# The last row tile of a feed-forward's second product as whole float32: a hybrid encoder on one Trainium2 core

## The chip, the core and the metric

The kernel runs on one core of a Trainium2 chip, in one launch. The metric is the device time of the launch in microseconds (us); the lower the better. A run is timed as a whole; beside it stands one profiled execution, whose trace gives every time of a single instruction in this text.

## The reference

Two layers of an encoder on 256 tokens of width 1024, all in float32. Cut to what matters here, a layer is

```python
def swiglu(x, w_in, w_out):
    h = x @ w_in                                   # 1024 x 5632
    gate, up = h[..., :D_FF], h[..., D_FF:]
    return (jax.nn.silu(gate) * up) @ w_out        # 2816 x 1024

x = layer_norm(ALPHA * x + 0.5 * swiglu(x, ffn1_w_in[l], ffn1_w_out[l]), ...)
mix = hybrid_mixer(x, ...)     # one input projection, two kinds of attention, one output projection
x = layer_norm(ALPHA * x + mix, ...)
x = layer_norm(ALPHA * x + 0.5 * swiglu(x, ffn2_w_in[l], ffn2_w_out[l]), ...)
```

So there are four feed-forwards. Each has a second product, `g @ w_out`, over D_FF = 2816 = 22 x 128 rows of `w_out`.

## The kernel before

**Split operands.** TensorE works here on a type called float32r, float32 of reduced precision. To keep precision, every operand of a large product is split in two: a high part (the value cast to float32r) and a low part (the value less its high part, cast again). A product is then the sum of three matmuls: high by high, high by low, low by high. For a weight tile of 128 rows and 1024 columns this is done by `Weights._make` (lines 64 to 76): a DMA on SyncE's queue brings the tile into a buffer `raw` (five buffers), ScalarE casts it into `wh` (line 74, nine buffers), VectorE subtracts into `wl` (line 75, nine buffers). Both are issued at low priority. `srcs` (lines 126 to 138) lists all weight tiles in the order of their use, and `W.get(i)` (lines 82 to 84) has the program name eight tiles more than the one asked for (`LOOK`); the DMAs go out in that order as buffers come free.

**A feed-forward** is `ffn` (lines 288 to 402). The first four column blocks of gate and up are made by `first` (line 301). The other 18 are made by `col` (lines 324 to 343): two PSUM tiles `hg` and `hu`, filled from 16 matmuls each (lines 334 and 335), are added up, put through Silu and multiplied, which gives `gv` (line 340), a block of 128 rows of g-transposed by 256 tokens in plain float32, in half of the buffer `tl`. Lines 342 (ScalarE) and 343 (VectorE) split it into `gs`, which holds all 22 blocks for the second product.

**The second product** runs over the 22 row tiles k of `w_out`, for two halves t of 128 tokens. `step` (lines 376 to 383) issues for one k and one t the three partial products into the accumulators `acc[t]`: two of 512 columns, but in the program's last feed-forward three for the second half (512, 256, 256). The first 15 tiles are taken for both halves at once. The last seven (`TAIL`) are taken for the first half, whose normalisation then starts, and afterwards for the second half; there the last three tiles (`SPLIT`) are taken accumulator by accumulator. Before the last three steps the first half of the normalised x is transposed for the next stage (`to_xt`, line 400).

**What sets the order.** TensorE's instructions run in the order in which the code issues them (`manual_schedule(engines={PE})`, line 112). For the other engines a planner orders the work at compile time, by the data that each instruction needs and by priority; it also decides which buffer of a pool a tile gets. Each engine then executes its list strictly in order. In the mixer TensorE's order is written out by hand in `ORDER` (lines 47 to 54). It begins with `P dk 0 1`, a part of the key projection, whose weights are the fifth tile behind the last one of `w_out`.

**Plain float32 elsewhere.** The attention's products of probabilities and values are not split: line 568 (`od<-vd,pTd`, 128 columns) and line 598 (`os<-vs,pTs`, 64 columns) multiply plain float32. `diff_pv` issues 8 such calls and runs four times, `swa_pv` issues 16 and runs four times.

Of the kernel before, what the change touches and what calls it, by code (L numbers as in the profile page):

```python
# [19 lines left out]
P = 128  # L20
# [4 lines left out]
JT = DFF // P  # L25
# [25 lines left out]
S d 1; P sq 0 1; A 0 0; S d 1; P sq 0 1; P sq 1 2; A 0 1; T sk 1; T sq 0; T sk 0; V 0; P sq 1 1; A 1 1;  # L51
A 1 0; S s 0; Y 0 0; P sq 1 1; G; O 0 1; V 1; S s 0; T sq 1; O 0 1; W 0 0; O 0 1; S s 1; W 0 1; W 0 2;
Y 1 0; S s 1; W 1 0; Y 0 1; O 0 1; O 1 1; O 0 2; W 1 1; W 1 2; O 0 2; Y 1 1; O 1 6; Z; O 1 1
"""


class Weights:


    def __init__(self, tc, pool, srcs):  # L60
        self.tc, self.nc, self.pool, self.srcs = tc, tc.nc, pool, srcs
        self.made = []

    def _make(self, i):
        nc = self.nc
        raw = self.pool.tile([P, 1024], F32, tag="raw", name=f"raw{i}", bufs=5)
        wh = self.pool.tile([P, 1024], F32R, tag="wh", name=f"wh{i}", bufs=9)
        wl = self.pool.tile([P, 1024], F32R, tag="wl", name=f"wl{i}", bufs=9)
        n = 512 if i == 0 else 1024
        for c in range(0, 1024, n):  # L70
            s = slice(c, c + n)
            nc.sync.dma_start(raw[:, s], self.srcs[i][:, s])
            with self.tc.high_priority(-LATER):
                nc.scalar.copy(wh[:, s], raw[:, s])  # L74
                nc.vector.tensor_tensor(wl[:, s], raw[:, s], wh[:, s].bitcast(F32), ALU.subtract)  # L75
        self.made.append((wh, wl))
# [11 lines left out]
def encoder_kernel(  # L88
# [22 lines left out]
    nc = tc.nc  # L111
# [10 lines left out]
    mm = nc.tensor.matmul  # L122
    dv = nc.vector


    srcs = []
    for l in range(DEPTH):
        srcs += [f1_b[l, k] for k in range(KT)]
        srcs += [f1_in[l, j, s] for j in range(JT - NB) for s in range(2)]
        srcs += [f1_out[l, k * P : (k + 1) * P, :] for k in range(JT)]  # L130
        for c in range(3):
            srcs += [m_in[l, c, q] for q in range(4)]
        srcs += [m_in2[l, q] for q in range(2)]
        srcs += [m_in[l, 3, q] for q in range(4)]
        srcs += [m_out[l, k * P : (k + 1) * P, :] for k in range(KT)]
        srcs += [f2_b[l, k] for k in range(KT)]
        srcs += [f2_in[l, j, s] for j in range(JT - NB) for s in range(2)]
        srcs += [f2_out[l, k * P : (k + 1) * P, :] for k in range(JT)]
    W = Weights(tc, wp, srcs)
    wi = 0  # L140


# [21 lines left out]
    for c in range(4):  # L164
        load_xt(c)
        W.upto(c + 1)
    x = []

    def load_x():
        for t in range(2):  # L170
            xt = xp.tile([P, D], F32, tag="x", name=f"x_in{t}")
            nc.sync.dma_start(xt, x_tok[t * P : (t + 1) * P, :])
            x.append(xt)
# [114 lines left out]
    def ffn(l, n, last=False):  # L288
        nonlocal wi
        nm = f"{l}{n}"  # L290
        gs = [gp.tile([P, 2, 2, SEQ], F32R, tag="g", name=f"g_{nm}_{q}") for q in range(JT // 2)]

        def first(ts, mid=None):

            hp = [[ps.tile([P, 512], F32, tag="b", name=f"hb_{nm}_{t}{s}") for s in range(2)] for t in ts]
            for k in range(KT):
                wh, wl = W.get(wi + k)
                for t, hb in zip(ts, hp):
                    for g, ww, e in ((0, wh, 0), (0, wl, 1), (1, wh, 2)):
                        for s in range(2):  # L300
                            mm(hb[s], xx[:, k, g, t, :], ww[:, 512 * s : 512 * s + 512],  # L301
                               start=(k == 0 and e == 0), stop=(k == KT - 1 and e == 2))
                if k == KT - 3 and mid is not None:
                    mid()
            out = []
            for t, hb in zip(ts, hp):
                sg = tp.tile([P, 512], F32, tag="tmp", name=f"sgb_{nm}_{t}")
                nc.scalar.activation(sg, hb[0], AF.Silu)
                gv = tp.tile([P, 512], F32, tag="tmp", name=f"gvb_{nm}_{t}")
                dv.tensor_tensor(gv, sg, hb[1], ALU.mult)  # L310
                out.append(gv)
            return out

        def first_t(gv, t):
            tr = ps.tile([P, 4, P], F32, tag="b", name=f"trg_{nm}{t}")
            for i in range(4):
                nc.tensor.transpose(tr[:, i, :], gv[:, i * P : (i + 1) * P], ident)
            for q in range(2):
                a = slice(t * P, (t + 1) * P)
                dh = gs[q][:, :, 0, a]  # L320
                nc.scalar.copy(dh, tr[:, 2 * q : 2 * q + 2, :])
                dv.tensor_tensor(gs[q][:, :, 1, a], tr[:, 2 * q : 2 * q + 2, :], dh.bitcast(F32), ALU.subtract)

        def col(j):
            nonlocal wi

            hs = [ps.tile([P, 2, SEQ], F32, tag="b", name=f"h{'gu'[s]}_{nm}_{j}") for s in range(2)]
            tl = tp.tile([P, 2, SEQ], F32, tag="tl", name=f"tl_{nm}_{j}", bufs=2)
            for s in range(2):
                wh, wl = W.get(wi)  # L330
                wi += 1
                for k in range(KT):
                    a = slice(k * P, (k + 1) * P)
                    mm(hs[s], wh[:, a], xx[:, k], start=(k == 0), stop=False)  # L334
                    mm(hs[s][:, 1, :], wl[:, a], xx[:, k, 0], start=False, stop=(k == KT - 1))  # L335
                nc.scalar.copy(tl[:, s], hs[s][:, 1, :])  # L336
                dv.tensor_tensor(tl[:, s], hs[s][:, 0, :], tl[:, s], ALU.add)  # L337
            nc.scalar.activation(tl[:, 0], tl[:, 0], AF.Silu)  # L338
            gv = tl[:, 1]
            dv.tensor_tensor(gv, tl[:, 0], gv, ALU.mult)  # L340
            q, jj = divmod(j, 2)
            nc.scalar.copy(gs[q][:, jj, 0, :], gv)
            dv.tensor_tensor(gs[q][:, jj, 1, :], gv, gs[q][:, jj, 0, :].bitcast(F32), ALU.subtract)

        first_x = l == 0 and n == 0
        if first_x:
            g0, g1 = first((0, 1))
        else:
            (g0,) = first((0,), lambda: to_xt(x[1], 1, f"x{nm}"))
            (g1,) = first((1,))  # L350
        wi += KT
        if not first_x:
            first_t(g0, 0)
        col(NB)
        if first_x:
            first_t(g0, 0)
        first_t(g1, 1)
        for j in range(NB + 1, JT):
            col(j)
            if first_x and j == NB + 2:  # L360
                load_x()
                rotary()
            if j == JT - 6:
                gb = load_gb(l, n)
                if n == 0:
                    load_mix(l)
        def cols(t, ws):
            out, o = [], 0
            for w in ws:
                out.append((slice(o, o + w), ps.tile([P, w], F32, tag="b", name=f"acc_{nm}_{t}{o}")))  # L370
                o += w
            return out

        acc = [cols(0, (512, 512)), cols(1, (512, 256, 256) if last else (512, 512))]

        def step(k, w, t, hs=None):
            wh, wl = w
            q, kk = divmod(k, 2)
            gh = gs[q][:, kk, 0, t * P : (t + 1) * P]
            gl = gs[q][:, kk, 1, t * P : (t + 1) * P]  # L380
            for g, ww, e in ((gh, wh, 0), (gh, wl, 1), (gl, wh, 2)):
                for s, a in acc[t] if hs is None else [acc[t][h] for h in hs]:
                    mm(a, g, ww[:, s], start=(k == 0 and e == 0), stop=(k == JT - 1 and e == 2))  # L383

        for k in range(JT - TAIL):
            w = W.get(wi)
            wi += 1
            for t in range(2):
                step(k, w, t)
        ws = []  # L390
        for k in range(JT - TAIL, JT):
            ws.append(W.get(wi))
            wi += 1
            step(k, ws[-1], 0)
        layer_norm(acc[0], 0, 0.5, gb, nm, last)
        todo = [(k, None) for k in range(JT - TAIL, JT - SPLIT)]
        todo += [(k, (h,)) for h in range(len(acc[1])) for k in range(JT - SPLIT, JT)]
        for i, (k, hs) in enumerate(todo):
            if i == len(todo) - TCUT and not last:
                to_xt(x[0], 0, f"y{nm}")  # L400
            step(k, ws[k - JT + TAIL], 1, hs)
        layer_norm(acc[1], 1, 0.5, gb, nm, last)
# [403 lines left out]
```

## Time and profile before

| | us |
|---|---|
| median of 3 runs (981.85 to 982.15) | 981.9 |
| the profiled execution | 980.99 |
| its span, first to last instruction | 978.8 |

The mean granted TensorE clock of the profiled execution was 0.998 of full speed. A page of the profile gives the busy time of each engine and, in 40 equal slices of the span, the share of each slice in tenths. PE is TensorE's matmuls, PEld its weight loads, DVE VectorE, ACT ScalarE, POOL GpSimd, SP SyncE (SPq its queue, which issues the DMAs). An instruction is named by its line in the kernel, its operation and its tiles, out<-in. Matmuls are pipelined, and their ends are modelled: the time from one start to the next tells what one costs, the shown length does not. The chain that ended last follows the work back from the last instruction, at each step to what released it; its rows give a start, a time, and what ran (x is the number of instructions).

### The profile page before, as it was taken

The page shows a single profiled execution, that of the slowest core. Times are in us where ns is not written, and L with a number is a line of the kernel's source. Part 1 is how long each engine was busy: PE and PEld are TensorE (multiplying, and loading weights), DVE is VectorE, ACT ScalarE, POOL GpSimd, SP SyncE. Part 2 cuts the span into 40 slices and gives each one's busy share as a digit, 9 for nine tenths or more (in the row PEclk, how much of TensorE's full clock was granted, in tenths as well). Part 3 has the DMA queues.
Part 4 walks back from the last instruction along what each step waited for, and adds up shares of the span by engine and source line. Part 5 has one row for each costly group of instructions (what it writes and reads, how often), then busy time and mean ns, then how long its engine had stood idle before and what let it go on. Part 6 is the DMA issues. An engine that isn't in the chain of part 4 may idle for free.

```text
span 978.8 us, 13934 instructions
## 1 busy us (share of the span) xinstructions
PE 966.7 (99%) x5199; PEld 820.0 (84%) x5199; DVE 664.6 (68%) x1057; ACT 510.5 (52%) x887; POOL 18.3 (2%) x30
## 2 busy tenths in 40 slices
PE   8999999999999999999999999999999999999997
PEld 5888888888888888888888888888888888888886
DVE  6886764698748766664587667548896587666534
ACT  4667553446745655553355555433575456555430
POOL 1000000000000000000000000000000000000000
PEclk9999999999999999999999999999999999999999
DMA  8885566365305755555376655563742176555511
GB/s 290 318 271 192 191 193 194 127 236 175 111 23 193 249 183 192 185 183 194 126 254 220 190 180 189 194 193 133 244 141 66 45 245 231 191 186 182 191 65 44
DMA packets 50323, 176.44 MB, mean 180 GB/s; under 512 B 5824, under 2 KB 7376, under 8 KB 50256
## 3 DMA queue, kind: packets, MB, share of 16 engines
q1 hardware_dynamic: 50192, 175.54, 53.9%
q8 instruction: 41, 0.67, 0.3%
q0 software_dynamic: 64, 0.02, 0.1%
q14 instruction: 26, 0.21, 0.1%
HBM read 174.48 MB, written 1.05 MB: 179 GB/s over the span
## 4 chain that ended last, share of the span: by engine, by line
PE 98%; DMA 1%; DVE 1%; SPq 0%; ACT 0%; issue 0%; DVEq 0%
PE acc L383 24%; PE hu L334 14%; PE hg L334 14%; PE hb L301 9%; PE hg L335 7%; PE hu L335 7%; PE ao L666 4%; PE ss L486 2%; PE os L598 1%; PE pj_sq L448 1%; DMA raw<-in_f_b_dram 1%; PE pj_sq L450 1%; PE pj_dq L450 1%; PE pj_dq L448 1%; PE pj_sq L449 1%; PE pj_dv L448 1%
## 5 line engine op out<-in xcount | busy, mean ns | idle before, releaser
L75 DVE TENSOR_TENSOR wl<-raw,wh 128x1024 fp32r<-128x1024 f32 (+1 forms) x317 | 385.4, 1220 | 206.5 <-ACT wh L74 203.2
L74 ACT CAST wh<-raw 128x1024 fp32r<-128x1024 f32 (+1 forms) x317 | 332.1, 1050 | 328.3 <-PE acc L383 126.8
L334 PE MATMUL hg<-xx,wh 128*128 128x512 f32 x576 | 206.3, 399 | 0.0
L334 PE MATMUL hu<-xx,wh 128*128 128x512 f32 x576 | 205.7, 398 | 0.0
L383 PE MATMUL acc<-wh,g 128*128 128x512 f32 (+1 forms) x748 | 192.7, 378 | 0.0
L335 PE MATMUL hg<-xx,wl 128*128 128x256 f32 x576 | 161.3, 280 | 0.0
L335 PE MATMUL hu<-xx,wl 128*128 128x256 f32 x576 | 161.3, 280 | 0.0
L383 PEld LDWEIGHTS acc<-wh,g 128*128 128x128 f32 x748 | 136.0, 188 | 25.9
L334 PEld LDWEIGHTS hu<-xx,wh 128*128 128x128 f32 x576 | 108.2, 188 | 26.5
L334 PEld LDWEIGHTS hg<-xx,wh 128*128 128x128 f32 x576 | 108.2, 188 | 26.1
L383 PE MATMUL acc<-wl,g 128*128 128x512 f32 (+1 forms) x374 | 111.4, 377 | 0.0
L335 PEld LDWEIGHTS hg<-xx,wl 128*128 128x128 f32 x576 | 108.8, 189 | 0.0
L335 PEld LDWEIGHTS hu<-xx,wl 128*128 128x128 f32 x576 | 108.7, 189 | 0.0
L383 PEld LDWEIGHTS acc<-wl,g 128*128 128x128 f32 x374 | 68.9, 188 | 13.2
L301 PE MATMUL hb<-wh,xx 128*128 128x512 f32 x256 | 70.8, 393 | 3.1 <-ACT wh L74 3.1
L301 PEld LDWEIGHTS hb<-wh,xx 128*128 128x128 f32 x256 | 47.9, 188 | 14.4 <-ACT wh L74 4.8
L301 PE MATMUL hb<-wl,xx 128*128 128x512 f32 x128 | 39.9, 392 | 0.5 <-DVE wl L75 0.5
L666 PE MATMUL ao<-wh,xx 128*128 128x512 f32 x128 | 37.7, 398 | 0.0
L340 DVE TENSOR_TENSOR tl<-tl 128x256 f32<-128x256 f32 x72 | 30.6, 425 | 9.5 <-ACT tl L338 2.4
L337 DVE TENSOR_TENSOR tl<-hu,tl 128x256 f32<-128x256 f32 x72 | 30.1, 418 | 0.5 <-ACT tl L336 0.5
L338 ACT ACTIVATE tl<-tl 128x256 f32<-128x256 f32 x72 | 30.3, 421 | 0.0
L337 DVE TENSOR_TENSOR tl<-hg,tl 128x256 f32<-128x256 f32 x72 | 30.1, 418 | 0.3 <-ACT tl L336 0.3
(184 smaller groups left out, 980.2 us busy)
## 6 DMA issues: line engine op xcount, KB each, us to landing
raw<-in_f_in_dram SPq DMA_DIRECT2D x144, 512.0 KB, 4.3
raw<-in_f_out_dram SPq DMA_DIRECT2D x88, 512.0 KB, 4.2
raw<-in_m_in_dram SPq DMA_DIRECT2D x36, 512.0 KB, 4.4
raw<-in_f_b_dram SPq DMA_DIRECT2D x31, 512.0 KB, 3.4
raw<-in_m_out_dram SPq DMA_DIRECT2D x16, 512.0 KB, 4.2
lng<-in_ln_g_dram SPq DMA_DIRECT2D x6, 512.0 KB, 5.6
lnb<-in_ln_b_dram SPq DMA_DIRECT2D x6, 512.0 KB, 5.9
xr<-in_x_tr_dram SPq DMA_DIRECT2D x4, 256.0 KB, 7.4
```

The source lines that it names most:

```text
L74: nc.scalar.copy(wh[:, s], raw[:, s])
L75: nc.vector.tensor_tensor(wl[:, s], raw[:, s], wh[:, s].bitcast(F32), ALU.subtract)
L301: mm(hb[s], xx[:, k, g, t, :], ww[:, 512 * s : 512 * s + 512], start=(k == 0 and e == 0), stop=(k == KT - 1 and e == 2))
L334: mm(hs[s], wh[:, a], xx[:, k], start=(k == 0), stop=False)
L335: mm(hs[s][:, 1, :], wl[:, a], xx[:, k, 0], start=False, stop=(k == KT - 1))
L337: dv.tensor_tensor(tl[:, s], hs[s][:, 0, :], tl[:, s], ALU.add)
L338: nc.scalar.activation(tl[:, 0], tl[:, 0], AF.Silu)
L340: dv.tensor_tensor(gv, tl[:, 0], gv, ALU.mult)
L383: mm(a, g, ww[:, s], start=(k == 0 and e == 0), stop=(k == JT - 1 and e == 2))
L448: mm(o, xx[:, k, 0, t, :], wh[:, s], start=(k == 0), stop=False)
L450: mm(o, xx[:, k, 1, t, :], wh[:, s], start=False, stop=(k == KT - 1))
L666: mm(acc[t][h], xx[:, k, g, t, :], ww[:, s], start=(k == 0 and e == 0), stop=(k == KT - 1 and e == 2))
```

## The change

For the last row tile, k = 21, of each of the four second products nothing is split. The weight tile stays in its `raw` buffer, and no `wh` and `wl` are made; the column block `gv` stays in `tl`, and lines 342 and 343 are left out for it. `step` then issues one matmul for each accumulator, with both operands in plain float32, instead of three on float32r parts.

```diff
@@ class Weights
+        self.whole = set()
 
     def _make(self, i):
         nc = self.nc
         raw = self.pool.tile([P, 1024], F32, tag="raw", name=f"raw{i}", bufs=5)
+        if i in self.whole:
+            nc.sync.dma_start(raw, self.srcs[i])
+            self.made.append((raw,))
+            return
         wh = self.pool.tile([P, 1024], F32R, tag="wh", name=f"wh{i}", bufs=9)
         wl = self.pool.tile([P, 1024], F32R, tag="wl", name=f"wl{i}", bufs=9)
...
-    srcs = []
+    srcs, whole = [], []
     for l in range(DEPTH):
...
         srcs += [f1_out[l, k * P : (k + 1) * P, :] for k in range(JT)]
+        whole.append(len(srcs) - 1)
...
         srcs += [f2_out[l, k * P : (k + 1) * P, :] for k in range(JT)]
+        whole.append(len(srcs) - 1)
     W = Weights(tc, wp, srcs)
+    W.whole.update(whole)
...
@@ col
             gv = tl[:, 1]
             dv.tensor_tensor(gv, tl[:, 0], gv, ALU.mult)
+            if j == JT - 1:
+                return gv
             q, jj = divmod(j, 2)
...
         for j in range(NB + 1, JT):
-            col(j)
+            gv = col(j)
...
         def step(k, w, t, hs=None):
+            if k == JT - 1:
+
+                for s, a in acc[t] if hs is None else [acc[t][h] for h in hs]:
+                    mm(a, gv[:, t * P : (t + 1) * P], w[0][:, s], start=False, stop=True)
+                return
             wh, wl = w
```

## Rows read from the trace of the kernel before

**Rows 1.** The page: span, busy time of the engines, and slices.
```profile
span 978.8 us, 13934 instructions
PE 966.7 (99%) x5199; PEld 820.0 (84%) x5199; DVE 664.6 (68%) x1057; ACT 510.5 (52%) x887; POOL 18.3 (2%) x30
...
PE   8999999999999999999999999999999999999997
...
PEclk9999999999999999999999999999999999999999
```

**Rows 2.** Waits of TensorE's matmuls: us in total, times, longest.
```profile
PE hb L301 <- ACT wh L74: 3.1, 3, 1.5
PE wps L154 <- DVE wz L151: 1.2, 1, 1.2
PE hb L301 <- DVE wl L75: 0.5, 1, 0.5
```

**Rows 3.** The page: the chain that ended last, by engine and by line.
```profile
PE 98%; DMA 1%; DVE 1%; SPq 0%; ACT 0%; issue 0%; DVEq 0%
PE acc L383 24%; PE hu L334 14%; PE hg L334 14%; PE hb L301 9%; PE hg L335 7%; PE hu L335 7%; PE ao L666 4%; PE ss L486 2%; PE os L598 1%; PE pj_sq L448 1%; DMA raw<-in_f_b_dram 1%; PE pj_sq L450 1%; PE pj_dq L450 1%; PE pj_dq L448 1%; PE pj_sq L449 1%; PE pj_dv L448 1%
```

**Rows 4.** The chain in order of time, around the second feed-forward's end.
```profile
428.65 57.87 PE acc L383 x255
486.51 0.87 PE tr_y L260 x8
487.39 2.06 PE acc L383 x9
489.44 8.16 PE hb L301 x36
```

**Rows 5.** Groups by line and shape, line 383: count, busy us, mean ns.
```profile
L383 PE MATMUL acc<-wh,g 128*128 128x512 f32 x660 | 184.8, 391 | 0.0
...
L383 PE MATMUL acc<-wl,g 128*128 128x512 f32 x330 | 105.2, 390 | 0.0
...
L383 PE MATMUL acc<-wh,g 128*128 128x256 f32 x88 | 17.3, 280 | 0.0
...
L383 PE MATMUL acc<-wl,g 128*128 128x256 f32 x44 | 9.3, 282 | 0.0
```

**Rows 6.** Timeline of TensorE, the kernel's last matmuls: start, us.
```profile
969.31 0.28 PE L383 MATMUL acc<-wl,g 128*128 128x256 f32 x1
...
971.11 0.28 PE L383 MATMUL acc<-wl,g 128*128 128x256 f32 x1
971.23 0.28 PE L383 MATMUL acc<-wh,g 128*128 128x256 f32 x1
```

**Rows 7.** Groups by line and shape, matmuls with 64 and 128 columns.
```profile
L598 PE MATMUL os<-vs,pTs 128*128 128x64 f32 x128 | 14.7, 274 | 0.0
...
L568 PE MATMUL od<-vd,pTd 128*128 128x128 f32 x64 | 7.8, 276 | 0.0
L525 PE MATMUL ss<-mask,identb 128*128 128x128 bf16 x32 | 7.4, 230 | 0.0
```

**Rows 8.** The chain in order of time, plain float32 in the first mixer.
```profile
249.24 1.80 PE od L568 x16
...
271.75 3.52 PE os L598 x32
```

**Rows 9.** Lines 568 and 598: lengths in ns (min/median/max), first and last start.
```profile
L568 PE MATMUL od<-vd,pTd x64: 270/275/292, 249.1 to 742.5; 128*128 128x128 f32 x64
...
L598 PE MATMUL os<-vs,pTs x128: 222/275/276, 271.6 to 771.2; 128*128 128x64 f32 x128
```

**Rows 10.** Timeline of VectorE at the end; the chain there.
```profile
971.55 0.42 DVE L271 SCALAR_TENSOR_TENSOR x<-acc,x 128x256 f32<-128x256 f32 x1
...
971.61 0.38 DVE x L271
```

**Rows 11.** Groups by line: the splitting of weights and of column blocks.
```profile
L75 DVE TENSOR_TENSOR wl<-raw,wh 128x1024 fp32r<-128x1024 f32 (+1 forms) x317 | 385.4, 1220 | 206.5 <-ACT wh L74 203.2
L74 ACT CAST wh<-raw 128x1024 fp32r<-128x1024 f32 (+1 forms) x317 | 332.1, 1050 | 328.3 <-PE acc L383 126.8
...
L343 DVE TENSOR_TENSOR g<-tl,g 128x256 fp32r<-128x256 f32 x72 | 30.1, 419 | 0.0
L342 ACT CAST g<-tl 128x256 fp32r<-128x256 f32 x72 | 28.8, 400 | 1.7 <-DVE tl L340 1.7
```

**Rows 12.** Timeline of SyncE's queue, first feed-forward; the page's median to landing.
```profile
157.19 0.33 SPq L72 DMA_DIRECT2D raw<-in_f_out_dram  x1
...
170.75 0.33 SPq L72 DMA_DIRECT2D raw<-in_m_in_dram  x1
...
raw<-in_m_in_dram SPq DMA_DIRECT2D x36, 512.0 KB, 4.4
```

**Rows 13.** Normalisation of the second half (VectorE's timeline), its transposes (the chain).
```profile
199.30 1.41 DVE L283 SCALAR_TENSOR_TENSOR x<-x,rs,lnb 128x512 f32<-128x512 f32 x2
...
201.91 0.87 PE tr_m L260 x8
```

## The prediction

> **What bounds the kernel now.** I read the page first: of a span of 978.8 us TensorE is shown busy for 966.7, and its clock is in the top tenth in all 40 slices [rows 1]. Busy time alone does not say that TensorE sets the end, so the waits come next: its matmuls wait for another engine for 4.8 us in the whole program, all in the warm-up and in the block product at line 301, never in the second product at line 383 [rows 2]. The chain that ended last agrees: 98% TensorE, a quarter of the span from line 383 alone [rows 3]. So what the change adds to or takes from TensorE's stream comes out in the time one for one, and what it takes from ScalarE, VectorE or the queues is worth nothing unless TensorE waited for it. The chain in order of time then gives the price of the matmuls concerned: 255 of them in 57.87 us, **227 ns** each at 512 columns [rows 4]. Durations will not do: the same matmuls are shown as 390 ns long [rows 5], because they overlap. In each of the first three feed-forwards the second product is one gapless run, interrupted only by the eight transposes before its last nine matmuls, and the next stage's matmuls follow without a gap [rows 4].
>
> **What the change removes from TensorE.** Line 383 runs once for each of three partial products (high by high, high by low, low by high). The last row tile (k = 21) needs, for each of two token halves, three matmuls for each accumulator. In three of the feed-forwards a half has two accumulators of 512 columns; in the fourth the second half has one of 512 and two of 256. That is 15 accumulators of 512 and 2 of 256, so 45 matmuls at 227 ns and 6 of 256 columns. The 256-column ones run 120 ns apart (15 matmuls from 969.31 to 971.11) [rows 6]. Removed: 45 x 227 + 6 x 120 = 10.9 us.
>
> **What it adds.** 17 matmul calls on plain float32. No call of that kind with 512 columns is in the trace, but two lines have it with fewer: line 568 (32 calls, 128 columns) and line 598 (64 calls, 64 columns). They show 64 and 128 records [rows 7], while the 1,122 calls of line 383 show 748 + 374 [rows 5]: a plain float32 call is **two** weight loads and two matmuls, where a float32r call is one. What I have to settle is how long one such record streams at 512 columns.
> - Spacing: 16 records of 128 columns take 1.80 us, 112.5 ns each; 32 of 64 columns take 3.52 us, 110 ns each [rows 8]. Half the columns save nothing, so at 64 columns something else, presumably the weight load, sets the pace, and at 128 columns it may do so too.
> - Length: from 512 to 256 columns of line 383 the shown length falls from 390 to 280 ns [rows 5], 0.43 ns per column. One pass over 128 columns should then show 225 ns, and the bfloat16 matmul of line 525 with 128 columns shows 230 [rows 7]. The float32 record with 128 columns shows 276 [rows 7], and two passes (256 columns) would show 280. At 64 columns the median is 275 too, but the shortest is 222 [rows 9]: two passes over 64 columns should show 225, one pass 198.
>
> So a float32 record fits two passes over its columns, a call four. The bounds: from below one pass in each record, 227 ns, so 454 for a call; from above the 112.5 ns of 128 columns taken four times, 450 ns, so 900. More is excluded, since no part of a record can cost more per column than the whole at 128. I take two passes, because both lengths are nearest to it. The slope of the float32r spacing is (227 - 120) / 256 = 0.42 ns per column, so 227 + 512 x 0.42 = 441 ns from the one side, and 112.5 + 768 x 0.42 = 434 from the float32 row itself; I take 437 ns for a record and 874 for a call. For 256 columns it is two passes over 256: between 227 and 112.5 + 107 = 220, so 223 and 446.
>
> The Trainium skill ("FP8 and Floating Point Precision", section "TensorE Precision Notes") says that true FP32 takes four passes through the array, and that reduced-precision FP32 is cut to 22 bits. That speaks against this change, which trades three passes for four; at 227 ns a pass it would give 15 x 227 = 3.4 us more, an estimate. The lengths above lean the same way, but no run here shows it at 512 columns.
>
> **The sum on TensorE.** For each 512-column accumulator 874 - 3 x 227 = +193 ns, 15 of them +2.9 us. For each 256-column one 446 - 360 = +86, together +0.17. The latter are the end of the kernel, where the first 0.1 us is covered: VectorE is still busy with the normalisation of the columns before, and starts on the last 256 at 971.55, when the last matmul (971.23, shown as 0.28 long) has been over for 0.04; by the chain it starts at 971.61 [rows 6, 10]. So +0.1. **Sum: +3.0 us** (2.8 to 3.5 between the two-pass ends).
>
> **Off TensorE.** For each of the four last tiles one cast (1.05 us of ScalarE) and one subtraction (1.22 us of VectorE) go, and for the last column block one copy (0.40) and one subtraction (0.42) [rows 11], 12.4 us of two engines. TensorE never waited for any of it [rows 2], so I cost it at nothing. The DMA is the same 512 KB in its old place on SyncE's queue.
>
> **What is held instead.** The raw tile is now freed by TensorE's last use of it, not by VectorE's subtraction. It occupies one of five raw buffers until the end of the feed-forward, but leaves one of nine wh and wl buffers to the next tile: the stock of loaded tiles stays at 14. Before, the last tile's DMA went out at 157.19 and the fifth one behind it at 170.75, when a cast and a subtraction had freed a raw buffer [rows 12]. After, the next tile takes that cast's place and frees its buffer at the same moment. The new wait of the matmul is for a landing some 4 us after issue [rows 12], 20 us before its use. Cost: nothing, as long as the pool gives a waiting load whichever buffer is free.
>
> **Rivals.**
> 1. *One pass in each record.* Then a call is 454 ns, the 512-column accumulators save 227 each, 15 x 227 = 3.4 us, and the end, set by VectorE, gains nothing there: **978.5**. For it: the spacings of rows 8 do not exclude it, if weight loads set both. Against: the 276 and the 222 above. The Trainium skill ("TensorE: Matmul & The Clock Gate", sections "LDWEIGHTS (loading the stationary operand)" and "Weight-path perf modes") has a load of 128 columns take 128 / 1.2 = 107 ns and no fast load for FP32; by that the 110 and 112.5 ns would be the load's price, and this case would stay open.
> 2. *Three passes*, the same three products that the kernel forms by hand: 227 + 437 = 664 against 681, -0.25 us, **981.6**. Against: the lengths of line 568 show no short and long records in turn (270 to 292, median 275) [rows 9].
> 3. *The held raw buffer starves the next stage* (slower by far more). If buffers go round in fixed order, the fifth load behind the whole tile waits for its last matmul. It holds the first weights that the mixer multiplies (key columns, fifth in the list). In place of 170.75 it would be issued at about 193.7, land 4.4 later [rows 12], be cast by 1.05 more, and the low part 1.2 after that, against 0.23 of work: a stall of 6.5 us in each of two mixers and about 1 us between the layers, **998** with the 3.0. It decides as soon as the load comes out behind the last matmul. Against: the code gives the pool a count of buffers and no order, so any free one may serve; the rows of before can't show it, since there buffers come free in the order in which they were filled.
> 4. *A shifted plan.* With two operations fewer the order of ScalarE's and VectorE's work may come out differently. The nearest cover is small: the second half's normalisation ends at 200.71 (199.30 and 1.41) and its transposes start at 201.91 [rows 13]. One subtraction more ahead of it (1.22) would use that up, so I allow about 1 us either way.
>
> **Numbers.** Chances: two passes 0.80, one pass 0.07, three passes 0.05, starvation 0.04, the rest 0.04. A measurement of this kernel can tell about 0.2%, 2.0 us, from no change. The two-pass case lies beyond that, except where a shifted plan gives a us back; most of the rest goes to the slower side: faster 0.07, within 0.2% 0.08, slower 0.85. The profiled execution took 980.99 us, 0.9 under the median of 981.9; to the first the sum gives 984.0, to the median **984.9**. The range takes the two-pass ends and about 1 us of shifted plan on each side: 981.9 + 2.8 - 1.2 = 983.5 and 981.9 + 3.5 + 1.2 = 986.6; I round outwards to 983.3 and 986.8. It leaves out the one-pass, three-pass and starvation cases, 0.16.
>
> **What would show it.** Line 383 should fall by 51 records and a new line show 34, the 512-column ones about 437 ns apart and some 600 ns long. The first three second products should be longer by about 0.77 us each, the stages between them unchanged, and the waits of TensorE still at 4.8 us. Spacings of 227 would prove rival 1, alternating ones rival 2, a wait of the mixer's first matmul for a cast rival 3. The prediction is wrong if the second products do not account for the difference.

## The result, and the profile after

| | before | after |
|---|---|---|
| median of 8 runs, us | 981.88 (980.72 to 982.15) | 983.76 (983.53 to 986.47) |
| the profiled execution, us | 980.99 | 983.72 |
| its span, us | 978.8 | 981.9 |

The ratio of the times is 1.0025, with a 95% interval of 1.0016 to 1.0034: the kernel became **slower**, by 2.5 us (1.6 to 3.3), a quarter of a per cent. The prediction was 984.9 in a range of 983.3 to 986.8, and +3.0 us. The spans of the two profiled executions differ by 3.1 us, their times by 2.7.

First the waits of TensorE's matmuls after the change (line numbers have moved: 301 is now 309, 383 is 398, and the new call is line 390; us in total, times, longest).

```profile
PE hb L309 <- ACT wh L79: 2.1, 3, 0.9
PE wps L162 <- DVE wz L159: 1.2, 1, 1.2
PE hb L309 <- DVE wl L80: 0.3, 1, 0.3
```

They are the same three as in [rows 2], 3.6 us in all. No new wait has appeared. Then the chain in order of time, around the second feed-forward's end as in [rows 4].

```profile
429.45 49.02 PE acc L398 x216
478.47 1.72 PE acc L390 x4
480.19 6.85 PE acc L398 x30
487.04 0.86 PE acc L390 x2
487.90 0.87 PE tr_y L268 x8
488.77 1.39 PE acc L398 x6
490.16 0.86 PE acc L390 x2
491.02 8.21 PE hb L309 x36
```

This stretch took 428.65 to 489.44 before, 60.79 us, and takes 429.45 to 491.02 now, 61.57: **+0.78**. Eight plain float32 records (four calls) stand in the place of twelve float32r ones: 1.72 us for four is 430 ns each. And there is a small change-over: 216 float32r matmuls run 226.9 ns apart, but the 30 behind the first float32 group take 6.85 us, 0.04 more than 30 x 226.9, and the six before the last pair 1.39, 0.03 more. Four accumulators at 4 x (860 - 681) = 0.72 us, and 0.07 for the changes, make the 0.78. A third change-over falls behind the stretch: the next stage's first 36 matmuls take 8.21 us, where they took 8.16 [rows 4]. The groups by line and shape (count, busy us, mean ns) show the records themselves.

```profile
L398 PE MATMUL acc<-wh,g 128*128 128x512 f32 x630 | 178.5, 393 | 0.0
L398 PE MATMUL acc<-wl,g 128*128 128x512 f32 x315 | 100.1, 390 | 0.0
L398 PE MATMUL acc<-wh,g 128*128 128x256 f32 x84 | 17.4, 286 | 0.0
L390 PE MATMUL acc<-raw,tl 128*128 128x512 f32 x30 | 14.7, 591 | 0.0
L398 PE MATMUL acc<-wl,g 128*128 128x256 f32 x42 | 8.7, 281 | 0.0
L390 PE MATMUL acc<-raw,tl 128*128 128x256 f32 x4 | 1.2, 378 | 0.0
```

Line 383's 1,122 matmuls [rows 5] have become 1,071, with 34 new ones beside them: 51 out, 34 in. The second products account for 2.9 of the 3.1 us of span: 0.78 us in each of the first three feed-forwards and 0.6 in the last. The stages between them are longer by 0.04 to 0.05 us each (234.90 to 234.94, 125.21 to 125.26 and 234.90 to 234.95 by the chain), another 0.14 in all; in the second of them it is the change-over just named.

The end of the kernel, by the chain:

```profile
973.51 0.71 PE acc L398 x6
974.22 0.45 PE acc L390 x2
974.67 0.02 issue
974.70 0.43 DVE x L279
```

Before, VectorE started on the last 256 columns when it had finished the columns before them [rows 10]; now it starts 0.02 us after TensorE's last matmul. So the 0.1 us of cover at the end was used up, as the sum had it.

What is held shows in SyncE's queue and in VectorE's order (timelines of the first feed-forward, and of the chain for the transposes).

```profile
170.73 0.33 SPq L77 DMA_DIRECT2D raw<-in_m_in_dram  x1
```

```profile
200.60 1.41 DVE L291 SCALAR_TENSOR_TENSOR x<-x,rs,lnb 128x512 f32<-128x512 f32 x2
```

```profile
202.72 0.87 PE tr_m L268 x8
```

The fifth load behind the last tile goes out at 170.73, where it went at 170.75 [rows 12]: it passes the held buffer by. The planner did shift VectorE's work: the second half's normalisation now ends at 202.01, 0.71 us before its transposes, where it had 1.20 before [rows 13]. That cost nothing, but a part of the cover is gone.

### The profile page after: what moved, and what is told of

It reads as the page before. It is cut to its first block, busy times and chain, and to the rows that moved or that the text cites. A ratio compares the mean times of both kernels' runs of the same rounds, so it can differ in the third digit from the quotient of the medians.

```text
span 981.9 us, 13870 instructions
## 1 busy us (share of the span) xinstructions
PE 971.1 (99%) x5182; PEld 817.5 (83%) x5182; DVE 659.7 (67%) x1049; ACT 505.2 (51%) x879; POOL 18.3 (2%) x30
## 4 chain that ended last, share of the span: by engine, by line
PE 98%; DMA 1%; DVE 0%; SPq 0%; ACT 0%; issue 0%; DVEq 0%
PE acc L398 23%; PE hu L342 14%; PE hg L342 14%; PE hb L309 9%; PE hg L343 7%; PE hu L343 7%; PE ao L681 4%; PE ss L501 2%; PE os L613 1%; PE acc L390 1%; PE pj_sq L463 1%; DMA raw<-in_f_b_dram 1%; PE pj_sq L465 1%; PE pj_dq L465 1%; PE pj_dq L463 1%; PE pj_sq L464 1%
## 5 line engine op out<-in xcount | busy, mean ns | idle before, releaser
L80 DVE TENSOR_TENSOR wl<-raw,wh 128x1024 fp32r<-128x1024 f32 (+1 forms) x313 | 380.5, 1220 | 206.9 <-ACT wh L79 203.9
L79 ACT CAST wh<-raw 128x1024 fp32r<-128x1024 f32 (+1 forms) x313 | 328.2, 1050 | 334.5 <-PE acc L398 127.5
L398 PE MATMUL acc<-wh,g 128*128 128x512 f32 (+1 forms) x714 | 186.6, 380 | 0.0
L398 PEld LDWEIGHTS acc<-wh,g 128*128 128x128 f32 x714 | 129.8, 188 | 26.7 <-issue 2.2
L398 PE MATMUL acc<-wl,g 128*128 128x512 f32 (+1 forms) x357 | 105.7, 378 | 0.0
L398 PEld LDWEIGHTS acc<-wl,g 128*128 128x128 f32 x357 | 65.7, 188 | 13.0 <-issue 0.2
```

## The experiments

All ratios are to the kernel before, run beside each kernel on the same chip (its medians there: 982.4 to 982.6 us). The executions of one kernel also differ at their start, which has nothing to do with the change: in e8's profiled execution the first matmuls behind the first wait for weights ran at the lower of the clock's two levels, 1.2 GHz (granted clock 0.50 in the stretch from 13.0 to 18.5 us), in that of before none did. I therefore also give, for the profiled execution, the span less the start of the first second product: 978.8 - 132.99 = 845.8 before and 981.9 - 132.97 = 848.9 after.

| | ratio, 95% interval | median, us | span from the first second product on, us |
|---|---|---|---|
| the change | 1.0025 (1.0016 to 1.0034) | 983.76 | 848.9 |
| e1, last tile by high parts alone | 0.9976 (0.9962 to 0.9991) | 979.83 | 980.8 - 134.08 = 846.7 |
| e2, float32 matmul, splitting kept | 1.0030 (1.0018 to 1.0042) | 984.72 | 982.0 - 134.40 = 847.6 |
| e3, pieces of 64 columns | 1.0171 (1.0156 to 1.0186) | 998.30 | 996.5 - 132.89 = 863.6 |
| e4, two tiles whole | 1.0064 (1.0047 to 1.0080) | 987.54 | 984.4 - 132.84 = 851.6 |
| e5, pieces of 256 columns | 1.0024 (1.0015 to 1.0034) | 984.92 | 983.2 - 134.41 = 848.8 |
| e6, four tiles held | 1.0147 (1.0129 to 1.0166) | 996.89 | 993.7 - 132.79 = 860.9 |
| e7, the same matmuls, nothing held | 1.0107 (1.0087 to 1.0127) | 993.27 | 992.9 - 135.73 = 857.2 |
| e8, e1 with another order | 0.9919 (0.9899 to 0.9940) | 973.99 | 974.8 - 136.05 = 838.8 |
| e9, that order alone | 1.0002 (0.9991 to 1.0013) | 982.13 | 978.8 - 133.03 = 845.8 |

### How long does a float32 record stream? e5 and e3

The two kernels are the changed one with its new matmul cut into pieces of n = 256 or n = 64 columns.

```diff
-                    mm(a, gv[:, t * P : (t + 1) * P], w[0][:, s], start=False, stop=True)
+                    for o in range(s.start, s.stop, n):
+                        mm(a[:, o - s.start : o - s.start + n], gv[:, t * P : (t + 1) * P],
+                           w[0][:, o : o + n], start=False, stop=(o + n == s.stop))
```

> The changed kernel with each 512-column plain float32 matmul cut into two of 256 columns. Theory, a record streams two passes over its columns and nothing is paid per call: 4 records of 215 ns (the spacing that the change showed at 256 columns) in place of 2 of 430, so the same time as the change within 0.3 us, and the longer second products unchanged. Rival, a call has a fixed price (its two weight loads): with 17 to 32 calls some 110 ns more for each added record, 30 x 0.11 = 3.3 us above the change.

> The changed kernel with each plain float32 matmul cut into pieces of 64 columns (8 for 512, 4 for 256). Theory, below 128 columns the weight load sets the pace at the 110 ns that line 598 showed: a 512-column accumulator takes 16 records x 110 = 1760 ns in place of 860, 15 x 0.9 + 2 x 0.45 = 14.4 us more than the change, about 998. Rival, the passes over the columns are all that counts and the 110 ns of line 598 had another cause: 16 x 59 = 944 ns, 1.3 us more, about 985.

The chain in order of time gives the spacings, for e5 and then for e3.

```profile
479.88 1.73 PE acc L391 x8
```

```profile
482.07 3.52 PE acc L391 x32
```

At 256 columns a record takes 1.73 / 8 = 216 ns, half of the 430 at 512, and the kernel's time is that of the change (848.8 against 848.9 in the last column). So between 512 and 256 columns nothing is paid per call, only per column: 256 columns more cost a record 430 - 216 = 214 ns, 0.84 ns each, where they cost a float32r matmul 227 - 120 = 107 ns, 0.42 each [rows 4, 6]. Twice the price per column is what two passes in each record would give. At 64 columns a record takes 110 ns, the spacing of line 598 [rows 8], and the kernel 998.3 where 998 was expected. Halving the columns from 512 to 256 halves a record, but at 64, an eighth, it does not go below 110. The price per column is thus shown from 256 to 512 columns, and the floor under it at 64. That the floor is the weight load is the likeliest reading, since every record brings a load of 128 columns of its own, however narrow it is (256 loads for 256 records in e3, 64 for 64 in e5); but no run here varies the weight load itself. The Trainium skill ("TensorE: Matmul & The Clock Gate", section "LDWEIGHTS (loading the stationary operand)") gives P / 1.2 ns for a load of P columns, so an estimate of 107 ns for 128, with which the 110 agrees.

### Is it TensorE's stream alone? e2

The splitting, the buffers and the off-engine work of the kernel before stay; only the last tile's matmul is the change's.

```diff
@@ step
+            if k == JT - 1:
+                for s, a in acc[t] if hs is None else [acc[t][h] for h in hs]:
+                    mm(a, gh.bitcast(F32), wh[:, s].bitcast(F32), start=False, stop=True)
+                return
             for g, ww, e in ((gh, wh, 0), (gh, wl, 1), (gl, wh, 2)):
```

> The kernel before, with all its splitting, buffers and plan, but for the last row tile one plain float32 matmul on the high parts gh and wh (their bits read as float32; the low parts are left out). So only TensorE's work changes, as in the change. Theory, the whole difference is TensorE's: 15 x (4 x 215 - 3 x 227) = 2.7 us and some 0.1 to 0.2 at the end, 984.7, the four second products longer by 0.78, 0.78, 0.78 and about 0.6 us in the trace as after the change. Rival, the held raw buffer or the shifted plan has a share in it, for good or ill: a difference from before that is more than 0.5 us away from that of the change in the profiled spans (+3.1).

The chain around its second feed-forward's end:

```profile
431.01 49.02 PE acc L387 x216
480.04 1.72 PE acc L383 x4
481.75 6.85 PE acc L387 x30
488.60 0.86 PE acc L383 x2
489.46 0.87 PE tr_y L260 x8
490.33 1.40 PE acc L387 x6
491.73 0.86 PE acc L383 x2
```

It is the change's stretch to within a hundredth, 61.58 us for 61.57, although here ScalarE and VectorE still do all of the 12.4 us that the change removes. The ratio, 1.0030, covers that of the change. So the difference is made by the matmuls, and the work taken off the other two engines is worth nothing, as costed. In the last column e2 stands 1.3 below the change. That comes from another place, the first product of the third feed-forward, which ran 1.7 us faster in this execution (last section). That its whole span (982.0) is so near the change's (981.9) is chance, since its first second product began 1.4 us later. Nor did the plan stay that of the kernel before, as the expectation had it. In the first feed-forward (VectorE's timeline, then the chain):

```profile
203.00 1.41 DVE L283 SCALAR_TENSOR_TENSOR x<-x,rs,lnb 128x512 f32<-128x512 f32 x2
```

```profile
204.15 0.97 PE tr_m L260 x8
```

Four of the weights' subtractions now stand between the operations of the second half's normalisation, where two stood before. It ends at 204.41, when its transposes have already begun, and these take 0.97 us in place of 0.87. So the plan shifts with TensorE's stream alone, and the shift costs 0.1 us here.

### What would a saving on TensorE have brought? e1, e8, e9

If TensorE's stream sets the time one for one, it should do so downwards too.

```diff
@@ step
+            if k == JT - 1:
+                for s, a in acc[t] if hs is None else [acc[t][h] for h in hs]:
+                    mm(a, gh, wh[:, s], start=False, stop=True)
+                return
             for g, ww, e in ((gh, wh, 0), (gh, wl, 1), (gl, wh, 2)):
```

> The kernel before, with the last row tile multiplied by high parts alone: one float32r matmul for each accumulator in place of three (the two products with a low part are left out; all splitting stays). Theory, TensorE's stream sets the time one for one and a matmul of 512 columns costs 227 ns: 15 accumulators save 2 x 227 ns each, 6.8 us, and the 256-column ones at the end save nothing, so 975.1 (ratio 0.993). Rival, something else than TensorE's stream sets part of the time around the last tile: a saving well under 6 us.

It saved 2.4 us by the ratio (0.9 to 3.7), not 6.8: the expectation **missed**. The waits of its matmuls name a place:

```profile
PE pj_dk L453 <- DVE wl L75: 4.1, 2, 2.1
PE hb L301 <- ACT wh L74: 3.0, 2, 2.5
```

The first key matmul with a low part waits 2.06 us in each of the two mixers. VectorE's timeline shows why: it had begun the second half's normalisation, and the subtraction for the fifth tile stands behind it. Here are its rows at the first mixer, in the kernel before and then in e1 (columns: start, us, then the instruction).

```profile
189.67 2.35 DVE L75 TENSOR_TENSOR wl<-raw,wh 128x1024 fp32r<-128x1024 f32 x2
```


```profile
193.44 0.68 DVE L271 SCALAR_TENSOR_TENSOR x<-acc,x_in 128x512 f32<-128x512 f32 x1
194.03 1.22 DVE L75 TENSOR_TENSOR wl<-raw,wh 128x1024 fp32r<-128x1024 f32 x1
```

Before, the fifth tile's subtraction is the second of the two at 189.67: it stood ahead of that work and was done at 192.02, 1.8 us before the matmul that needs it (193.81). In e1 the planner put five operations ahead of it, and it runs from 194.03. In the old order it would have been done at about 192.2 (an estimate: 189.86, where the one before it starts, and 2.35 for the two), before the matmul could start at 193.09. So it is a shifted plan, rival 4 of the prediction, that made the wait, and not the fewer matmuls alone. The order is the same in the second mixer.

The wait costs a second time. Here is TensorE in the stretches before, around and behind it (busy us and count of PE, PEld, DVE, ACT and POOL, then the granted clock, the DMA share and GB/s).

```profile
183.10:192.80 9.70, 9.70 (x48) 8.12 (x47) 9.44 (x15) 5.94 (x7) 0.93 (x1) 1.00 0.23 68
192.86:196.60 3.74, 1.68 (x8) 1.05 (x7) 3.74 (x6) 2.33 (x3) 0.00 (x0) 1.00 0.31 112
196.75:200.10 3.35, 3.35 (x10) 2.61 (x9) 3.35 (x7) 0.00 (x0) 0.99 (x1) 0.51 0.88 301
200.20:203.00 2.80, 2.80 (x14) 2.27 (x13) 2.80 (x4) 0.00 (x0) 0.00 (x0) 1.00 0.95 326
```

Shortly behind the wait the granted clock is 0.51, the 1.2 GHz level, for 3.4 us, and the matmuls stand 0.43 us apart there, not 0.23. It is back at 1.00 from 200.2 on. Two waits of 2.1 us and two stretches of 3.4 us at half speed (1.6 to 1.7 us lost in each) make some 7 us. In the profiled execution (982.54 us) the saving is gone altogether (846.7 against 845.8); e1's times spread from 977.95 to 983.01.

To show that this wait, and not something else, took the missing gain, e8 lets TensorE begin the mixer with other weights, which are split earlier:

```diff
-P dk 0 1; P dq 0 3; P dk 0 2; X;
+P dq 0 3; P dk 0 3; X;
```

> e1 again (last row tile by high parts alone), with the mixer's hand-written order begun by the query projection's first three parts, whose weights are split earlier, and the key projection's first part put behind them. e1 saved 2.4 us where 6.8 were due; in its trace the mixers' first key matmul waited 2.06 us for VectorE's subtraction, and the matmuls after it ran at half the granted clock for some 3.4 us. Theory, VectorE, strictly in order, holds the low part of the fifth tile behind the normalisation, and this wait and the lower clock behind it took the missing 4.4 us: without the wait 975 to 976, no wait for a subtraction in the mixer, granted clock 1.00 there. Rival, the missing time lies elsewhere: 979.8 as in e1.

> The kernel before with e8's order of the mixer's first parts and nothing else, a control for e8. Theory, before the change no matmul of the mixer waits for a subtraction, so there is no wait to remove: the same as before within 0.2%, 981.5 to 983, and e8's gain over e1 is the wait alone. Rival, the order is worth something by itself: 2 us or more under before, as a part of e8's gain.

e8 takes 0.9919 of the time (0.9899 to 0.9940), 974.0 us; its matmuls wait for nothing in the mixer, and the same place now reads:

```profile
194.80:203.00 8.20, 8.20 (x38) 6.71 (x37) 8.20 (x14) 2.38 (x3) 0.99 (x1) 1.00 0.64 206
```

By the ratio that is 8.0 us (5.9 to 9.9), and from the first second product on it is 845.8 - 838.8 = 7.0 us under the kernel before, where 6.8 were due. e9, the order without the saving, is 1.0002 (0.9991 to 1.0013): nothing by itself. So the price on TensorE holds in both directions, as long as no shift of VectorE's order makes the next stage wait. e8 is the fastest kernel here, though it leaves out two of the last tile's three partial products, and so is no substitute for either kernel.

### Does holding raw buffers cost anything? e4, e6, e7

e4 makes the last two tiles whole instead of one (`whole += range(len(srcs) - 2, len(srcs))`, and `k >= JT - 2` where `k == JT - 1` stood).

> The changed kernel with the last two row tiles whole in place of one, so two raw buffers are held to the end of each feed-forward. Theory, only TensorE's passes count: twice the change's difference, about +5.5 us over before (5.4 for 30 accumulators of 512 and some 0.1 to 0.2 at the end), 987.4, and TensorE's waits unchanged at about 4 us. Rival, holding raw buffers starves the next stage: more than 7 us over before, and a wait of the mixer's first matmuls, or of the next block product, for a cast.

1.0064 (1.0047 to 1.0080), 5.8 us in the last column. Thirty accumulators at 0.179 us make 5.4 of it; the rest, 0.4, is left for the 256-column ones and the change-overs, which are no more than in the change, so that it is a little under twice the change's 3.1. The waits are unchanged.

```profile
PE hb L309 <- ACT wh L79: 2.8, 2, 2.2
PE wps L162 <- DVE wz L159: 1.2, 1, 1.2
PE hb L309 <- DVE wl L80: 0.3, 1, 0.3
```

e6 goes to the limit and holds four of the five, e7 runs the same matmuls on split tiles.

```diff
@@ e6, on the changed kernel
-        whole.append(len(srcs) - 1)
+        whole += range(len(srcs) - 4, len(srcs))
@@ step
+            if k >= JT - 4:
+                q, kk = divmod(k, 2)
+                gv = gs[q][:, kk, 0, t * P : (t + 1) * P].bitcast(F32)
+                for s, a in acc[t] if hs is None else [acc[t][h] for h in hs]:
+                    mm(a, gv, w[0][:, s], start=False, stop=(k == JT - 1))
+                return
@@ e7, on the kernel before: step as in e2, with k >= JT - 4
```

> The changed kernel with the last four weight tiles whole (multiplied with the high part of g read as float32; the products with the low part of g are left out). Four of five raw buffers are held to the end of each feed-forward, and all later loads go through one. Theory A, only the stock of loaded tiles counts and it stays at 14: four times the price of one tile, 60 x 0.179 us + some 0.4 at the end, 11.1 us over before, 993, with TensorE's waits at about 4 us. Theory B, one buffer is too few (a load takes 0.4 + 4 + 1.05 + 1.22 = 6.7 us through it against 2.7 us of use): waits of TensorE for casts or subtractions at the start of the mixer or of the next block product, 2 us or more in all above e7.

> The kernel before with the last four row tiles as one plain float32 matmul on the high parts (bits read as float32, the low parts left out), split and buffered as before: the same matmuls as e6 with nothing held. By both theories 11.1 us over before, 993; the difference of e6 from it is the price of holding four buffers.

e7 gives 993.27 us, where 993 was expected, so the price of a tile adds up. e6 is 3.6 us above it, with intervals apart: here theory A **fell**. The waits of e6 that e7 does not have:

```profile
PE pj_dk L464 <- DVE xx L271: 1.2, 1, 1.2
...
PE hb L309 <- DVE xx L271: 0.8, 1, 0.8
PE tr_x L268 <- DVE x L291: 0.6, 1, 0.6
...
ACT wh L79 <- DMA raw<-in_m_in_dram: 60.5, 15, 5.7
```

They are not the waits that theory B named. The chain shows what goes through the one buffer left:

```profile
176.59 1.06 ACT wh L79
177.68 1.24 DVE wl L80
178.93 3.46 DMA raw<-in_m_in_dram
```

ScalarE's casts wait for loads that come one at a time (60.5 us in 15 waits), VectorE's subtractions wait for the casts, and behind the subtractions, in VectorE's order, stand the normalisation and the new xx, for which TensorE waits. By the chains the two mixers, each with the second product before it, are 2.6 and 0.8 us longer than in e7, and the second feed-forward with the block product behind it 2.0, which is 5.4; the third feed-forward's faster first product (last section) takes 1.7 of that back. So it is not the stock of loaded tiles alone that matters but the buffers left to turn over: four (the change) and three (e4) are enough, one is not, and two were not tried.

## Why the prediction was right

- *TensorE sets the time.* Right: e2 has the change's matmuls with all the splitting and buffers of the kernel before, and gives the change's second products to within a hundredth and a ratio that covers its own; e7 and e4 add up per tile. That less work on TensorE also comes out one for one holds only with e8's order: in e1 a wait that was not there before took most of it.
- *45 + 6 matmuls out, 10.9 us.* Right: 51 records fewer, still 227 ns apart.
- *A call is two records, each of two passes.* Right in the price: from 256 to 512 columns a record pays twice per column what a float32r matmul pays (e5). The predicted record of 437 ns measures 430 at 512 columns and 215 at 256 (predicted 223); its shown length is 591 ("some 600"). Of the bounds, one pass (227) is out, and so are three (no short and long records in turn). The argument from the shown lengths at 64 and 128 columns carried this step; the spacings of [rows 8] were at the floor, as said.
- *The sum, +3.0.* Close, and in part by luck. The terms were a little too high for the records (34 x 7 ns = 0.24) and left out the change-over between the two kinds of matmul (0.07 in each feed-forward and 0.04 to 0.05 behind each of the first three, 0.4 in all); the two errors go opposite ways. So a feed-forward takes 0.78 us more, where 0.77 was predicted, and the last 0.6. The span grew by 3.1 us, the time by 2.5 in the ratio and by 1.9 in the median.
- *Nothing off TensorE.* Right, by e2.
- *Nothing for the held buffer.* Right for one buffer and for two (e4), for the reason given: the fifth load went out at the same moment. It would not have been right for four (e6), and then not through the wait that rival 3 named. (Rival 3's 998 counts its 17 us from the profiled 981.0, where the other rivals start from the median; from that it would be 999.)
- *The shifted plan, rival 4.* It happened: VectorE's order changed, and 0.5 us of its cover went, at no price here. The reason given, two operations fewer, is not needed for it: the order shifts in e2 and e1 too, where all of them stay. What such a shift can cost is more than the 1 us allowed: in e1 it made the two waits.
- The Trainium skill ("FP8 and Floating Point Precision", section "TensorE Precision Notes") has four passes for true FP32. The 860 ns for a call of 512 columns against 227 for one float32r matmul, 3.8 times, are near that.

## What to carry to other kernels

Before two operands are kept whole to save their splitting, count the passes of the matmul that takes them: here plain float32 cost 860 ns for 512 columns against 681 for three float32r matmuls, and all the splitting that it saved lay beside TensorE's work and was free. Where one engine carries 98% of the chain, as TensorE does here, added time on it came out one for one, but a saving came out only when the plan of the other engines did not shift against it; compare the order of the engine that feeds the next stage, before and after, ahead of counting on a gain. A buffer held longer cost nothing as long as the others could turn over at the rate of use: here three of five left were enough, one was not.

## What the runs showed that was not expected

- **A 2 us wait costs nearly twice.** In e1 TensorE had run without a gap before it waited 2.06 us, in both mixers; 1.3 and 0.6 us after it had started again, the granted clock fell to 0.51 and 0.50, and it came back 3.4 us later.
- **Two rhythms of the same stream.** From the end of the block product to the second product, the chain's third feed-forward takes 512.12 to 614.65 before and 513.75 to 616.28 after the change, 102.53 us in both, but 515.42 to 616.24 in e2 and 522.35 to 623.17 in e6, 100.82. TensorE runs the same 576 matmuls there in the same order without a wait and at a granted clock of 1.00, about 353 ns from one pair of lines 334 and 335 to the next in the one case and 347 in the other. The other runs, e7 among them, all have the slower rhythm there. What sets it was not tried; 1.7 us is more than half of the effect studied here, so a profiled span alone would have misled for e2 and e6.
- **The start differs from run to run.** The first second product began between 132.8 and 136.1 us in the profiled executions. The granted clock was 0.50 from 13.0 to 18.5 us in e8:

```profile
13.00:18.50 5.50, 5.46 (x12) 3.86 (x13) 5.37 (x8) 3.26 (x4) 0.00 (x0) 0.50 1.01 397
```
